# An encoder trunk on one core: the order of each engine's instructions, taken from one scheduling turn and a table of rank changes

## The chip, the cores and the metric

The kernel runs on one core of a Trainium2 chip. A core has five engines with an instruction queue each: TensorE (PE, matrix products), VectorE (DVE), ScalarE (ACT), GpSimd (POOL) and SyncE (SP, which here starts transfers). The metric is the device time of one execution in microseconds (us), lower is better. Of the kernel before there are three timed runs and one profiled execution.

## The reference

Two layers work on an input of 512 rows of 1024 numbers in float32. Each layer normalizes, mixes the rows by attention, normalizes and adds; then it normalizes, runs a gated feed-forward block, normalizes and adds:

```python
for layer in range(2):
    h = rms_norm(x, norm_mix_pre[layer])
    h = neighbourhood_attention(h, ...) if layer == 0 else dilated_attention(h, ...)
    x = x + rms_norm(h, norm_mix_post[layer])
    h = rms_norm(x, norm_ffn_pre[layer])
    x = x + rms_norm(swiglu(h, w_gate, w_up, w_down), norm_ffn_post[layer])
# swiglu(h) = (silu(h @ w_gate) * (h @ w_up)) @ w_down, inner width 2816
```

Layer 0 lays the rows on an 8 x 64 grid; each of 16 heads of 64 attends to a window of 8 grid rows by 16 columns, with a learned bias by relative position. Layer 1 has three attentions side by side, each with its own queries, keys and values: windows of 128, 512 and 2048 over every row, every 4th and every 16th, with a penalty by distance; their outputs are weighted by their softmax denominators and summed.

## The kernel before

**Products.** A float32 product is made of three faster ones: each operand is split into a high part (ScalarE copies it rounded, L437) and a low part (VectorE subtracts, L438), and `mm3` issues high x high, high x low and low x high (L449, L450, L451). Large products are cut into 2 x 2 blocks and made from seven block products ("units") instead of eight. The sums of weight blocks that this needs are made on POOL or VectorE (L517 to L523), their splits on ScalarE and VectorE. ScalarE (L529, L752, L758, L765) and VectorE (L753, L760, L763) read the finished sums from PSUM, the memory where TensorE accumulates.

**Stages of a layer.** q, k and v (products `vp`, `pp_n` in layer 0, `vd`, `pp_d` in layer 1); attention of a pair of heads; the output product `yo`; gate and up products `gu`; the down product `yd`. In between, rows are normalized: ScalarE squares and sums (L708), VectorE multiplies (L709), POOL raises the mean to the power -1/2 (L657), VectorE scales and adds the residual (L715), and the next pre-norm squares on ScalarE (L662), uses POOL's L657 again, and scales on VectorE (L664). `transposed` then turns four 128 x 128 blocks on TensorE into one PSUM bank (L671, `tr_...`), ScalarE copies the high part out (L673) and VectorE the low part (L674). The names `h_a`, `l_a` are the two parts of a weight block, `rxa`, `rxb`, `rxc` the parts of the transposed rows.

**Attention of layer 1.** In a pair `j`, `scores_a` makes the scores of the widest neighbourhoods as split products (`sa`, L1330); `scores_b` makes those of the other two attentions as plain float32 matmuls on 64 rows (`sb`, L1350). A softmax follows (VectorE L1313, ScalarE L1314). ScalarE scales the result by the weights of the three attentions in 128 x 256 pieces (L1400), TensorE transposes them (`t1_j`, L1410), four to a bank; ScalarE copies one bank out and VectorE the next (both L1411). `values` multiplies with v, again in plain float32 (`o1`, L1419). Layer 0 has plain float32 products too (`o`, L845). VectorE also splits the rotated q and k (L774, L780 to L785).

**Buffers.** PSUM has eight banks, in four uses: three for `pp` (units), two for scores, two for transposes ("t"), one for attention outputs. The third tile of a use waits until the readers of the first are done.

**What sets the order.** The code records all instructions and does not run in the order in which it is written. `Order` collects them with their dependences (data, buffers) and a cost of its own for each. `run(rank, back)` is a list scheduler: each of five queues (four engines and SyncE's transfers) takes, whenever it is free, the ready instruction of lowest rank; TensorE prefers to stay with the kind of matmul it is in when a rank is less than 1000 ns behind (`stay`). Run backwards from the end, it gives new ranks. `pin` alternates forward and backward in 20 turns. It then rates the 20 orders with `usual`, the mean length of an order under three draws of random delays; it starts from the best, and for each stretch of 100 us it tries the ranks of 12 other turns and keeps a mixture that rates better. At last it ties each instruction to the one ahead of it on its engine, so the order found at build time is the order on the chip.

Of the kernel before, what the change touches and what calls it, by code (L numbers as in the profile page):

```python
# [70 lines left out]
def _in_psum(b):  # L71
    return list(b.tensor.shape) == [P, 512]
# [6 lines left out]
def _cost(i, e):  # L79
# [8 lines left out]
    if t == "InstDMACopy":  # L88
        adds = "bypass" not in str(getattr(i, "cce_op", "bypass"))
        size = 4 * n * outs[0].ap[0][1] * (1.78 if adds else 1)  # L90
# [9 lines left out]
    if e == 1:  # L100
        f = str(getattr(i, "func", ""))
        if "Exp" in f or "Silu" in f or len(srcs) > 1 and n > 16:
            c = 55 + 1.38 * n
        else:
            c = (48 if _in_psum(srcs[0]) else 80) + 0.86 * n
        c += _scattered(outs[0]) * 0.95 * n
        return (c + 93, c + 290, False, 0, 0) if len(outs) > 1 else (c, c + 100, False, 0, 0)
    if e == 2:
        c, lock = 60 + 1.055 * n, sum(not _in_psum(b) for b in srcs) > 1
        if t == "InstMemset":  # L110
            return 180, 270, False, 0, 0
        if t == "InstTensorCopy":
            lock = not _in_psum(srcs[0])
            c = 60 + (0.53 if lock else 1.055) * n
        elif t == "InstCustomDveAnt":
            c, lock = c + 90, False
        elif t == "InstTensorScalarPtr" and n == D:
            c = 1202
        c += _scattered(outs[0]) * 0.78 * n
        return c, c + 80, lock, 0, 0  # L120
    if e == 3:
        if t == "InstMemset":
            return 30 + n, 60 + n, False, 0, 0
        if t == "InstTensorTensor":
            c = 515 if n == 1 else 90 + 2.28 * n
        else:
            c = 300 + 0.62 * n if t == "InstTensorScalarPtr" else 260
        return c, c + 40, True, 0, 0
    return 100, 100, False, 0, 0


class Order:
# [147 lines left out]
                now = min(q[0] if q is wake else q[0][0] for q in (wake, pending) if q)  # L280
        return starts, order, max(s + max(c[1], c[4] and LANDING + c[4] / RATE) for s, c in zip(starts, self.costs))

    def through(self, order, costs):

        left, ready, at, last = [len(p) for p in self.pred], [0.0] * len(self.all), [0] * 5, 0.0
        free, locked, half, kind, pipe = [0.0] * 5, [0.0] * 5, [0.0] * 2, 0, 0.0
        rest = [e for e in range(5) if order[e]]
        while rest:
            now, e, k = min((max(free[e], ready[order[e][at[e]]]), e, order[e][at[e]]) for e in rest
                            if not left[order[e][at[e]]])  # L290
            taken, later, lock, mode, size = costs[k]
            s = max(now, pipe - AHEAD) if e == 4 else max(now, locked[5 - e]) if lock else now
            if e == 0:
                if mode > 2:
                    s = max(s + SWITCH.get((kind, 3), 0), half[mode - 3])
                    half[mode - 3] = s + later - 200
                else:
                    s = max(s + SWITCH.get((kind, mode), 0), max(half) + 95)
                    taken += 100 * (kind == 3)
                kind = min(mode, 3)  # L300
            if lock:
                locked[e] = s + taken
            if size:
                pipe = max(s + taken, pipe) + size / RATE
                end = pipe + LANDING + later
            else:
                end = s + later
            free[e], last = s + taken, max(last, end)
            for v in self.succ[k]:
                same = self.engine[v] == e and not size  # L310
                ready[v] = max(ready[v], s + taken if same and e == 0 else end if same else end + SYNC)
                left[v] -= 1
            at[e] += 1
            if at[e] == len(order[e]):
                rest.remove(e)
        return last

    def usual(self, order):

        ends = []  # L320
        for seed in range(3):
            r, costs = random.Random(seed), []
            for e, (taken, later, lock, mode, size) in zip(self.engine, self.costs):
                if size:
                    later = r.gauss(300, 700) if size < 4e5 else r.gauss(50, 800)
                    later *= 1.6 if e == 3 else 1
                else:
                    later += r.expovariate(1 / 15)
                costs.append((taken, later, lock, mode, size))
            ends.append(self.through(order, costs))  # L330
        return sum(ends) / len(ends)

    def pin(self, tc, times, span):
        rank, found = list(range(len(self.all))), []

        self.costs = [(t, LATE if 0 < size < 2e4 else later, lock, mode, size) for t, later, lock, mode, size in self.costs]
        for _ in range(times):
            starts, order, end = self.run(rank, False)
            found.append((self.usual(order), end, rank, starts, order))
            starts, _, end = self.run([-s - c[1] for s, c in zip(starts, self.costs)], True)  # L340
            rank = [end - s - c[0] for s, c in zip(starts, self.costs)]
        found.sort(key=lambda f: f[0])

        best, end, rank, base, order = found[0]
        for lo in np.arange(0.0, max(base), span):
            part = [k for k, s in enumerate(base) if lo <= s < lo + span]
            for _, _, other, _, _ in found[1:13]:
                mixed, shift = list(rank), float(np.median([rank[k] - other[k] for k in part]))
                for k in part:
                    mixed[k] = other[k] + shift  # L350
                _, new, e = self.run(mixed, False)
                usual = self.usual(new) if e < end + 3000 else best
                if usual < best:
                    best, end, rank, order = usual, e, mixed, new
        for q in order:
            for m, n in zip(q, q[1:]):
                tc.add_manual_dep(self.all[n], self.all[m].name,
                                  mybir.DependencyInfo(mybir.DependencyClass.NoSync, mybir.DependencyReason.DATA),
                                  reason="order")
# [3 lines left out]
def encoder_kernel(ctx: ExitStack, tc: tile.TileContext, a: dict, out: bass.AP):  # L363
# [1069 lines left out]
    order = [3 * j + g for j in range(PAIRS) for g in orders[j]]  # L1433
    stats, parts, weight, pts, vg, ready, left, later = {}, {}, {}, {}, {}, [], {}, {}

    vus, vslots = {}, cycle([hl(rxc[:, 24:], 0, D), hl(rxs, 2, D), (vmem, rxs[:, 4 * D:])])
    for qd in range(2):
        v = v_quarter(ap[:, (6 + qd) * D:(7 + qd) * D], a["dil_v"][0, qd], f"d{qd}")
# [75 lines left out]
              for n, lo, hi, o, c, side in arenas]  # L1514
    order = Order(tc.nc.cur_bb.bb.instructions)
    order.link(tags, places, extra)
    order.pin(tc, 20, 1e5)


def _blocks(w, cols):  # L1520
# [79 lines left out]
```

## Time and profile before

| | |
|---|---|
| median of 3 runs | 1460.94 us (1460.33 to 1461.76) |
| the profiled execution | 1460.49 us |
| its span, first to last instruction | 1458.7 us |
| TensorE clock granted, mean | 0.997 |
| busy: PE matmul | 1423.1 us, 98% of the span, 10788 instructions |
| busy: PE weight load | 1318.6 us, 90% |
| busy: DVE | 1179.3 us, 81%, 1876 instructions |
| busy: ACT | 902.1 us, 62%, 1819 instructions |
| busy: POOL | 541.0 us, 37%, 398 instructions |
| read from and written to HBM | 229.24 MB and 68.29 MB, 204 GB/s over the span |

The profiled execution's own time is 1.79 us over its span and 0.45 us under the median of the runs. Busy time is the sum of the times in which an engine works on something. The matmul's end is modelled and successive matmuls overlap, so PE can read as fully busy while its starts lie further apart than they need to. The distance between starts is what tells.

### The profile page before, as it was taken

How to read it: one execution, taken by the hardware profiler on the slowest of the kernel's cores; microseconds unless marked ns; L12 is line 12 of the kernel's file. 1: busy time of each engine (PE TensorE's matmuls, PEld its weight loads, DVE VectorE, ACT ScalarE, POOL GpSimd, SP SyncE). 2: the span in 40 equal slices, each digit the busy share in tenths (PEclk: the TensorE clock that was granted, in tenths of full speed). 3: DMA queues.
4: the chain of work that ended last, by engine and by line, in shares of the span. 5: the costliest groups of instructions: out<-in, count | busy, mean ns of one | idle time of the engine just before them, and what ended most of it. 6: DMA issues, size and time to landing. Idle time of an engine off the chain costs nothing.

```text
span 1458.7 us, 27918 instructions
## 1 busy us (share of the span) xinstructions
PE 1423.1 (98%) x10788; PEld 1318.6 (90%) x10788; DVE 1179.3 (81%) x1876; ACT 902.1 (62%) x1819; POOL 541.0 (37%) x398
## 2 busy tenths in 40 slices
PE   7999999999999999999999999999999999999997
PEld 6998877999999888999999999999877999999886
DVE  5499976899999888878678678787667989998877
ACT  4478873655555657544477677887775645555664
POOL 5345524544430001765553433344213644340001
PEclk9999999999999999999999999999999999999999
DMA  5356578788234674445433343343675788944662
GB/s 204 125 196 166 186 249 215 257 240 219 99 117 142 198 231 164 156 154 173 131 105 102 111 139 95 97 146 117 218 222 201 212 213 259 269 151 152 200 218 95
DMA packets 86645, 253.22 MB, mean 174 GB/s; under 512 B 19312, under 2 KB 31600, under 8 KB 84464
## 3 DMA queue, kind: packets, MB, share of 16 engines
q1 hardware_dynamic: 77696, 197.69, 41.0%
q0 software_dynamic: 8672, 53.48, 14.3%
q8 instruction: 85, 1.39, 0.4%
q14 instruction: 48, 0.39, 0.1%
q10 hardware_dynamic: 144, 0.26, 0.0%
HBM read 229.24 MB, written 68.29 MB: 204 GB/s over the span
## 4 chain that ended last, share of the span: by engine, by line
PE 82%; DVE 7%; ACT 5%; issue 2%; DMA 1%; POOL 1%; SPq 0%; POOLq 0%; DVEq 0%; ACTq 0%
PE gu L449 9%; PE gu L450 9%; PE gu L451 9%; PE pp_d L449 4%; PE pp_d L450 4%; PE pp_d L451 4%; PE yd_s L451 3%; PE yd_s L449 3%; PE yd_s L450 3%; PE vd L449 2%; PE vd L450 2%; PE vd L451 2%; PE yd_pp L451 2%; PE yd_pp L449 2%; PE yd_pp L450 2%
## 5 line engine op out<-in xcount | busy, mean ns | idle before, releaser
L657 POOL TENSOR_TENSOR rs_yd<-v_yd,mhalf 128x1 f32<-128x1 f32 x8 | 13.2, 1654 | 259.0 <-DVE v_yd L655 259.0
L450 PE MATMUL gu<-rxc,h_a 128*128 128x256 f32 x352 | 98.9, 281 | 1.3 <-DVE rxc L674 1.3
L449 PE MATMUL gu<-rxc,h_a 128*128 128x256 f32 x352 | 98.4, 280 | 1.0 <-ACT h_a L437 0.7
L449 PE MATMUL gu<-rxa,h_c 128*128 128x256 f32 x352 | 98.6, 280 | 0.6 <-DVE mem L915 0.4
L451 PE MATMUL gu<-rxc,l_a 128*128 128x256 f32 x352 | 98.6, 280 | 0.1
L449 PE MATMUL gu<-rxa,h_b 128*128 128x256 f32 x352 | 97.9, 278 | 0.1
L451 PE MATMUL gu<-rxa,l_b 128*128 128x256 f32 x352 | 97.7, 278 | 0.2 <-DVE l_b L438 0.2
L450 PE MATMUL gu<-rxa,h_b 128*128 128x256 f32 x352 | 97.8, 278 | 0.0
L450 PE MATMUL gu<-rxa,h_c 128*128 128x256 f32 x352 | 97.6, 278 | 0.0
L451 PE MATMUL gu<-rxa,l_c 128*128 128x256 f32 x352 | 97.4, 278 | 0.0
L517 POOL TENSOR_TENSOR r_d<-r_d 128x512 f32<-128x512 f32 x24 | 35.2, 1465 | 163.3 <-DVE l_ad L438 131.3
L437 ACT ACTIVATE rxc<-mem 128x512 fp32r<-128x512 f32 (+2 forms) x90 | 55.7, 623 | 60.7 <-PE yd_pp L450 32.0
L517 POOL TENSOR_TENSOR r_gu<-r_gu 128x512 f32<-128x512 f32 x20 | 33.3, 1666 | 153.0 <-DVE l_a L438 79.4
L438 DVE TENSOR_TENSOR rxc<-mem,rxc 128x512 fp32r<-128x512 f32 (+2 forms) x90 | 64.9, 727 | 16.8 <-ACT rxc L437 16.6
L517 POOL TENSOR_TENSOR raw<-raw 128x512 f32<-128x512 f32 x24 | 40.7, 1696 | 76.2 <-DVE l_a L438 73.5
L450 PEld LDWEIGHTS gu<-rxc,h_a 128*128 128x128 f32 x352 | 66.9, 190 | 1.7 <-DVE rxc L674 1.7
L449 PEld LDWEIGHTS gu<-rxc,h_a 128*128 128x128 f32 x352 | 66.8, 190 | 1.5 <-ACT h_a L437 1.0
L449 PEld LDWEIGHTS gu<-rxa,h_c 128*128 128x128 f32 x352 | 66.2, 188 | 1.6 <-DVE mem L915 0.6
L451 PEld LDWEIGHTS gu<-rxc,l_a 128*128 128x128 f32 x352 | 66.8, 190 | 0.3 <-DVE l_a L438 0.3
L449 PEld LDWEIGHTS gu<-rxa,h_b 128*128 128x128 f32 x352 | 66.3, 188 | 0.4 <-ACT h_b L437 0.3
L451 PEld LDWEIGHTS gu<-rxa,l_b 128*128 128x128 f32 x352 | 66.2, 188 | 0.4 <-DVE l_b L438 0.4
L450 PEld LDWEIGHTS gu<-rxa,h_b 128*128 128x128 f32 x352 | 66.2, 188 | 0.3 <-DVE rxa L674 0.2
(609 smaller groups left out, 6114.2 us busy)
## 6 DMA issues: line engine op xcount, KB each, us to landing
wsum<-wd POOLq DMA_DIRECT2D x24, 1408.0 KB, 11.9
r_d<-dil_qk SPq DMA_DIRECT2D x48, 512.0 KB, 4.0
raw<-wg SPq DMA_DIRECT2D x24, 512.0 KB, 5.0
raw<-wu SPq DMA_DIRECT2D x24, 512.0 KB, 7.0
wsum<-wsum POOLq DMA_DIRECT2D x8, 1408.0 KB, 10.5
raw<-wsum SPq DMA_DIRECT2D x22, 512.0 KB, 4.3
r_gu<-wg SPq DMA_DIRECT2D x20, 512.0 KB, 4.8
r_gu<-wu SPq DMA_DIRECT2D x20, 512.0 KB, 5.6
```

The lines of the kernel that those rows point to most:

```text
L437: act.activation(h, src, AF.Copy)
L438: dve.tensor_sub(l, src, h.bitcast(F32))
L449: i = pe.matmul(o, s[0], m[0], start=start, stop=False, skip_group_check=True)
L450: pe.matmul(o, s[0], m[1], start=False, stop=False, skip_group_check=True)
L451: pe.matmul(o, s[1], m[0], start=False, stop=stop, skip_group_check=True)
L517: self.added = e[0].tensor_add(q[0], q[0], q[2])
L657: pool.tensor_tensor(r, v, mhalf, op=ALU.pow)
```

## The change

The rating of orders is gone from the build: `through`, `usual` and the mixing by stretches. `pin` still makes 20 turns. It then takes the ranks of turn 5 and edits them by a table of 80 rows `(what, engine, lo, hi, turn, by)`. A row picks instructions of one engine (0 is PE, 1 ACT, 2 DVE; 5 is all) by their start in turn 5 (`what` 0 and 1, ns) or by their number (`what` 2). It adds `by` to their rank, or, for `what` 0, puts turn `turn`'s rank plus `by` in its place. One run of the scheduler with the edited ranks gives the order, which is tied as before. No instruction, transfer, buffer or dependence of the program's own is added or taken away.

```diff
-    def through(self, order, costs):
...
-    def usual(self, order):
...
+FIRST, TABLE = 5, (
+    (1, 0, 543664, 559242, 0, 1876), (2, 0, 5180, 5342, 0, 4228), (1, 0, 1022772, 1028275, 0, 1433),
...
-    def pin(self, tc, times, span):
+    def pin(self, tc, times, first, table):
...
-            starts, order, end = self.run(rank, False)
-            found.append((self.usual(order), end, rank, starts, order))
-            starts, _, end = self.run([-s - c[1] for s, c in zip(starts, self.costs)], True)
+            starts, _, end = self.run(rank, False)
+            found.append((rank, starts))
+            starts, _, _ = self.run([-s - c[1] for s, c in zip(starts, self.costs)], True)
             rank = [end - s - c[0] for s, c in zip(starts, self.costs)]
-        found.sort(key=lambda f: f[0])
-
-        best, end, rank, base, order = found[0]
-        for lo in np.arange(0.0, max(base), span):
-            part = [k for k, s in enumerate(base) if lo <= s < lo + span]
-            for _, _, other, _, _ in found[1:13]:
-                mixed, shift = list(rank), float(np.median([rank[k] - other[k] for k in part]))
-                for k in part:
-                    mixed[k] = other[k] + shift
-                _, new, e = self.run(mixed, False)
-                usual = self.usual(new) if e < end + 3000 else best
-                if usual < best:
-                    best, end, rank, order = usual, e, mixed, new
+
+        rank, base = list(found[first][0]), found[first][1]
+        for what, e, lo, hi, turn, by in table:
+            for k, s in enumerate(base):
+                if e in (5, self.engine[k]) and lo <= (k if what == 2 else s) < hi:
+                    rank[k] = by + (found[turn][0][k] if what == 0 else rank[k])
+        order = self.run(rank, False)[1]
...
-    order.pin(tc, 20, 1e5)
+    order.pin(tc, 20, FIRST, TABLE)
```

What it moves is seen in the order itself. A row below is a line of the source, the operation, out<-in and the shape; "x4" is four in a row. Lines of the changed source are 23 lower (L671 is L648 there, L449 to L451 are L426 to L428, L1410 is L1387). PE's first 131 and last 447 instructions stand as before; between them nearly every stretch differs, mostly by a few microseconds of work.

**First place: from the output product to the gate product of layer 0.** On PE, before; `yo0_3_1` is the last output block, `tr_o0_...` are transposes of normalized rows, `gu0_...` gate and up units:

```order
L449 MATMUL yo0_3_1_2708<-rxb0_92,rxa_77 128x512
L450 MATMUL yo0_3_1_2708<-rxb0_92,rxa_77 128x512
L451 MATMUL yo0_3_1_2708<-rxb0_92,rxa_77 128x512
L671 MATMUL tr_o0_0_0_2616<-ident_69,mem_79 128x128 x4
L671 MATMUL tr_o0_0_1_2623<-ident_69,mem_79 128x128 x4
L671 MATMUL tr_o0_1_0_2630<-ident_69,mem_79 128x128 x4
L671 MATMUL tr_o0_1_1_2637<-ident_69,mem_79 128x128 x4
L449 MATMUL gu0_0_2861<-rxc_78,h_a0_0_2862 128x256
L449 MATMUL gu0_1_2896<-rxc_78,h_a0_1_2897 128x256
L449 MATMUL gu0_2_2930<-rxc_78,h_a0_2_2931 128x256
L450 MATMUL gu0_0_2861<-rxc_78,h_a0_0_2862 128x256
L451 MATMUL gu0_0_2861<-rxc_78,l_a0_0_2863 128x256
```

The same on PE in the changed kernel:

```order
L426 MATMUL yo0_3_1_2708<-rxb0_92,rxa_77 128x512
L648 MATMUL tr_o0_0_0_2616<-ident_69,mem_79 128x128 x4
L648 MATMUL tr_o0_0_1_2623<-ident_69,mem_79 128x128 x2
L427 MATMUL yo0_3_1_2708<-rxb0_92,rxa_77 128x512
L428 MATMUL yo0_3_1_2708<-rxb0_92,rxa_77 128x512
L648 MATMUL tr_o0_0_1_2623<-ident_69,mem_79 128x128 x2
L648 MATMUL tr_o0_1_0_2630<-ident_69,mem_79 128x128 x4
L426 MATMUL gu0_0_2861<-rxc_78,h_a0_0_2862 128x256
L648 MATMUL tr_o0_1_1_2637<-ident_69,mem_79 128x128 x4
L426 MATMUL gu0_1_2896<-rxc_78,h_a0_1_2897 128x256
L427 MATMUL gu0_0_2861<-rxc_78,h_a0_0_2862 128x256
L428 MATMUL gu0_0_2861<-rxc_78,l_a0_0_2863 128x256
```

Two of the last output matmuls now stand behind the first transposes, and the first matmul of `gu0_2` no longer stands ahead of the rest of `gu0_0`: it follows 54 matmuls later.

On DVE at the same place, before:

```order
L674 TENSOR_TENSOR rxc_78<-tr_o0_0_0_2616,rxc_78 128x4x128
L709 TENSOR_TENSOR mem_79<-yo0_3_1_2708,mem_79 128x512
L674 TENSOR_TENSOR rxc_78<-tr_o0_0_1_2623,rxc_78 128x4x128
L715 SCALAR_TENSOR_TENSOR mem_79<-mem_79,few_small_80 128x1024
L674 TENSOR_TENSOR rxc_78<-tr_o0_1_0_2630,rxc_78 128x4x128
L674 TENSOR_TENSOR rxc_78<-tr_o0_1_1_2637,rxc_78 128x4x128
L438 TENSOR_TENSOR l_a0_2_2932<-raw0_2857,h_a0_2_2931 128x1024
```

And in the changed kernel:

```order
L651 TENSOR_TENSOR rxc_78<-tr_o0_0_0_2616,rxc_78 128x4x128
L632 TENSOR_SCALAR few_small_80<-few_small_80 128x1
L686 TENSOR_TENSOR mem_79<-yo0_3_1_2708,mem_79 128x512
L651 TENSOR_TENSOR rxc_78<-tr_o0_0_1_2623,rxc_78 128x4x128
L651 TENSOR_TENSOR rxc_78<-tr_o0_1_0_2630,rxc_78 128x4x128
L692 SCALAR_TENSOR_TENSOR mem_79<-mem_79,few_small_80 128x1024
L651 TENSOR_TENSOR rxc_78<-tr_o0_1_1_2637,rxc_78 128x4x128
L630 TENSOR_SCALAR few_small_80<-few_small_80 128x1
L641 SCALAR_TENSOR_TENSOR mem_79<-mem_79,few_small_80 128x1024
L415 TENSOR_TENSOR l_a0_2_2932<-raw0_2857,h_a0_2_2931 128x1024
```

The third low-part copy (of `tr_o0_1_0`) now stands ahead of the residual step (L715 before, L692 now), and the low part of the weight block `l_a0_2` behind the pre-norm's L664 (now L641). On POOL the L657 that the residual step needs has moved ahead of two 128 x 512 sums (L699, L701).

**Second place: pair 3 of layer 1's attention, about 882 us.** On PE, before; `sb_3_...` are plain float32 scores, `t1_2_...` transposes of pair 2, `pp_d14` a unit:

```order
L1350 MATMUL sb_3_0_1_9673<-mem_79 128x128 x2
L1410 MATMUL t1_2_9541<-ident_69,mem_79 128x128
L1410 MATMUL t1_2_9547<-ident_69,mem_79 128x128
L1410 MATMUL t1_2_9541<-ident_69,mem_79 128x128 x3
L1410 MATMUL t1_2_9547<-ident_69,mem_79 128x128 x3
L1350 MATMUL sb_3_0_1_9673<-mem_79 128x128 x2
L449 MATMUL pp_d14_9822<-rxa_77,h_ad14_9846 128x256
L1410 MATMUL t1_2_9609<-ident_69,mem_79 128x128
L1350 MATMUL sb_3_1_1_9674<-mem_79 128x128 x4
```

In the changed kernel:

```order
L1387 MATMUL t1_2_9541<-ident_69,mem_79 128x128 x4
L1327 MATMUL sb_3_0_1_9673<-mem_79 128x128 x4
L427 MATMUL pp_d14_9822<-rxa_77,h_ad14_9846 128x256
L428 MATMUL pp_d14_9822<-rxa_77,l_ad14_9847 128x256
L1387 MATMUL t1_2_9547<-ident_69,mem_79 128x128 x4
L1387 MATMUL t1_2_9609<-ident_69,mem_79 128x128
```

The scores of `sb_3_0_1` stand in one run instead of two; those of `sb_3_1_1` still make one of their own further on. Counted over the whole program, PE's plain float32 matmuls (`sb`, `o`, `o1`) stand in 76 separate runs before and 61 now: 26 and 22 for `sb`, 30 and 21 for `o1`, 20 and 18 for `o`. Runs of transposes number 108 and 112.

**Third place: pair 4, about 970 us.** On ACT, before; L1400 are the scalings, L1411 the copy out of a transpose bank, L778 and L779 q and k:

```order
L1400 ACTIVATE mem_79<-mem_79 128x256 x7
L1411 COPY mem_79<-t1_4_10626 128x512
L1400 ACTIVATE mem_79<-mem_79 128x256 x2
L778 ACTIVATE rxc_78<-memc0_2853 64x512
L1400 ACTIVATE mem_79<-mem_79 128x256 x3
L1411 COPY mem_79<-t1_4_10642 128x512
L779 ACTIVATE rxc_78<-memc0_2853 64x512
```

In the changed kernel:

```order
L1377 ACTIVATE mem_79<-mem_79 128x256 x8
L1388 COPY mem_79<-t1_4_10626 128x512
L1377 ACTIVATE mem_79<-mem_79 128x256 x2
L755 ACTIVATE rxc_78<-memc0_2853 64x512
L756 ACTIVATE rxc_78<-memc0_2853 64x512
L1377 ACTIVATE mem_79<-mem_79 128x256 x3
L1388 COPY mem_79<-t1_4_10642 128x512
```

Ahead of the copy of `t1_4_10642` stand, counted from the start of the program, three more scalings (the piece shows one of them), and L779. On PE the first transpose of `t1_4_10710`, which is the next to use the bank that this copy frees, follows the last transpose of `t1_4_10642` after 9 unit matmuls and six `sb` ones; before, after 37 and eight. Over all 32 such copies, counted from the start, 11 now have one to four more scalings ahead of them (24 in sum), 19 as many as before and 2 one fewer.

More of the change, by code (lines that the diff above doesn't have):

```diff
@@ L1 @@
 import heapq
-import random
 from contextlib import ExitStack, contextmanager
@@ L129, in _cost @@
     return 100, 100, False, 0, 0
+FIRST, TABLE = 5, (
[27 rows of a table added]
+)
 class Order:
@@ L281, in run @@
         return starts, order, max(s + max(c[1], c[4] and LANDING + c[4] / RATE) for s, c in zip(starts, self.costs))
-    def through(self, order, costs):
[L285 to L316, printed above, removed]
@@ L318, in usual @@
-    def usual(self, order):
[L320 to L331, printed above, removed]
```

26 rows, old and new, of the table c are left out of this document.

## The prediction

> **What bounds the kernel now.** I read the page's busy line and its chain first, then TensorE's waits, then PE's timeline, for the distances between starts.
>
> ```profile
> span 1458.7 us, 27918 instructions
> PE 1423.1 (98%) x10788; PEld 1318.6 (90%) x10788; DVE 1179.3 (81%) x1876; ACT 902.1 (62%) x1819; POOL 541.0 (37%) x398
> PE 82%; DVE 7%; ACT 5%; issue 2%; DMA 1%; POOL 1%; SPq 0%; POOLq 0%; DVEq 0%; ACTq 0%
> ...
> PE tr_a L671 <- DVE mem L664: 8.6, 2, 8.2
> PE sa L1330 <- DVE mem L1313: 1.3, 1, 1.3
> PE yo L449 <- DVE mn L817: 1.2, 1, 1.2
> ...
> PE s L805 <- POOL rxc L1199: 0.7, 1, 0.7
> ```
>
> PE is busy in 98% of the span and carries 82% of the chain. The waits (total us, times, longest) are small: the largest, 8.6, lies mostly ahead of the first transpose, where PE's order stays. No work goes away, so what an order can win is a few us: these waits, and distances between starts that the kind of neighbour sets. It can lose any amount, by new waits. 1% would be 14.6 us.
>
> **Term 1: fewer switches into plain float32.** PE's plain float32 matmuls (`sb`, `o`, `o1`) stand in 61 runs, not 76. What a run costs, PE's timeline shows (two trace rows per such matmul, so x4 is two matmuls and x8 four):
>
> ```profile
> 881.46 0.28 PE L450 MATMUL pp_d<-rxa,h_ad 128*128 128x256 f32 x1
> 881.57 0.28 PE L451 MATMUL pp_d<-rxa,l_ad 128*128 128x256 f32 x1
> 881.78 0.71 PE L1350 MATMUL sb<-mem 64*128 64x128 f32 x4
> ...
> 884.79 1.16 PE L1350 MATMUL sb<-mem 64*128 64x128 f32 x8
> 885.88 0.66 PE L1410 MATMUL t<-ident,mem 128*128 128x128 f32 x4
> ...
> 970.16 0.71 PE L1350 MATMUL sb<-mem 64*128 64x128 f32 x4
> 970.79 0.39 PE L451 MATMUL pp_d<-rxa,l_cd 128*128 128x256 f32 x1
> ```
>
> Unit matmuls start 0.11 apart (881.46, 881.57); into the float32 run it takes 0.21, so entering costs 0.10. Two matmuls hold PE from 970.16 to 970.79, 0.63; four from 884.79 to 885.88, 1.09. So one costs 0.23, and 1.09 - 4 x 0.23 = 0.17 is for leaving. A run costs 0.27. Output products leave more dearly:
>
> ```profile
> 197.65 0.54 PE L845 MATMUL o<-mem 128*64 128x192 f32 x2 [0.29 <-ACT mem L835]
> 198.12 0.50 PE L449 MATMUL yo<-h_wo,rxa 128*128 128x512 f32 x1
> ```
>
> One matmul takes 0.47 to the next start; less the 0.23 of the other shape (the nearest row), 0.24, so with entry 0.34 a run. Of the 15 runs fewer, 4 are `sb`, 11 outputs: 4 x 0.27 + 11 x 0.34 = 4.8. I take 15 x 0.30 = **-4.5**; ends 15 x 0.27 = 4.1 and 15 x 0.34 = 5.1. The four more runs of transposes I take at nothing: at 0.10 for an entry they would cost 0.4 at most. PE is the bound around these places, so the whole counts, unless PE would wait there anyway: then nothing.
>
> **Term 2: waits with more room.** The best shown is the way from the output product to the gate product of layer 0, from PE, DVE and POOL:
>
> ```profile
> 254.67 0.65 PE L671 MATMUL tr_o<-ident,mem 128*128 128x128 f32 x4 [1.18 <-DVE rxc L674]
> 255.87 0.66 PE L671 MATMUL tr_o<-ident,mem 128*128 128x128 f32 x4 [0.54 <-DVE rxc L674]
> 257.51 0.38 PE L449 MATMUL gu<-rxc,h_a 128*128 128x256 f32 x1 [0.75 <-ACT h_a L437]
> 258.67 0.58 PE L450 MATMUL gu<-rxc,h_a 128*128 128x256 f32 x1 [0.77 <-DVE rxc L674]
> ...
> 253.93 0.69 DVE L674 TENSOR_TENSOR rxc<-tr_o,rxc 128x512 fp32r<-128x512 f32 x1 [0.27 <-ACT rxc L673]
> 256.72 1.28 DVE L715 SCALAR_TENSOR_TENSOR mem<-mem,few_small 128x1024 f32<-128x1024 f32 x1 [0.91 <-POOL few_small L657]
> 257.93 1.28 DVE L674 TENSOR_TENSOR rxc<-tr_o,rxc 128x512 fp32r<-128x512 f32 x2
> 261.97 2.31 DVE L664 SCALAR_TENSOR_TENSOR mem<-mem,few_small 128x1024 f32<-128x1024 f32 x1 [0.44 <-POOL few_small L657]
> ...
> 256.14 0.55 POOL L657 TENSOR_TENSOR few_small<-few_small,mhalf 128x1 f32<-128x1 f32 x1
> ```
>
> The last number in brackets is PE's idle time and who ended it: 1.18, 0.54, 0.75 and 0.77. PE resumes at 258.67 when the copy of `tr_o0_1_0` is done, which stood behind L715, which waited for POOL. In the new order `tr_o0_0_0` starts two 512-wide matmuls earlier (0.23 each, 0.45); its L673, L674 follow at 253.5, L674 ends at 254.15, `tr_o0_1_0` goes at 254.2. On DVE come L709, L674 and then at once L674 of `tr_o0_1_0`, 0.6 apart: it ends near 256.2. So `gu0_0` goes on at 256.3, not 258.67, and 23 matmuls of `gu0_0` and `gu0_1` are at hand before `gu0_2` is asked for: about **-2.2**, after 0.1 to 0.2 for `gu0_2`'s moved matmul. What is late next: `l_a0_2` now stands behind L664 (2.31), but its user comes about 6 us after 256.3, and POOL's L657 comes two sums earlier, which brings L715 and L664 forward. The two sums themselves come 0.55 later (L657's time), and their transposes stand further back. Ends: -3.2 (all four waits) and 0.
>
> The others, by PE's idle times:
>
> ```profile
> 200.19 0.33 PE L830 MATMUL ta<-ident,mem 128*128 128x128 f32 x1 [0.65 <-POOL mem L1215]
> 737.71 0.35 PE L1330 MATMUL sa<-rxc 128*128 128x256 f32 x1 [1.27 <-DVE mem L1313]
> 751.98 0.39 PE L449 MATMUL pp_d<-rxa,h_cd 128*128 128x256 f32 x1 [0.46 <-DVE mem L763]
> 774.27 0.38 PE L451 MATMUL pp_d<-rxa,l_ad 128*128 128x256 f32 x1 [0.73 <-DVE l_ad L438]
> 779.05 0.39 PE L449 MATMUL pp_d<-rxa,h_cd 128*128 128x256 f32 x1 [0.30 <-DVE mem L763]
> 820.87 0.39 PE L449 MATMUL pp_d<-rxb,h_cd 128*128 128x256 f32 x1 [0.32 <-DVE mem L760]
> 1124.35 0.38 PE L450 MATMUL gu<-rxc,h_a 128*128 128x256 f32 x1 [0.51 <-DVE rxc L674]
> ```
>
> - End of layer 0's attention (197.65, 200.19): output matmuls now stand as filler ahead of both waits: -0.9 (0.29 + 0.65).
> - 738: more units stand ahead of `sa`, so its wait for the score bank goes, but L774, which it needs too, now stands behind a split on DVE: I take -0.5 of 1.27.
> - 752, 774, 779, 820: the producer named (L763, or `l_ad`) moves up on DVE, or a dozen unit matmuls come ahead: -1.5 of 1.81.
> - 1124, the same passage as the first, in layer 1: here L709 and L715 move ahead of the copies on DVE, the other way: +0.4, between a later wait gone (about 0.7) and 1.28 more.
>
> Sum: -2.2 - 0.9 - 0.5 - 1.5 + 0.4 = **-4.7**; ends -7.3 (all of these waits but the last) and 0.
>
> **Term 3: new waits in layer 1's attention.** Eleven of the 32 copies of a transpose bank by ACT now have more scalings ahead, 24 in sum. ACT's timeline:
>
> ```profile
> 969.33 1.29 ACT L1400 ACTIVATE mem<-mem 128x256 f32<-128x256 f32 x3
> 970.53 0.56 ACT L1411 COPY mem<-t 128x512 f32<-128x512 f32 x1
> 971.12 0.63 ACT L779 ACTIVATE rxc<-memc 64x512 fp32r<-64x512 f32 x1
> 976.27 1.06 ACT L437 ACTIVATE h_ad<-r_d 128x1024 fp32r<-128x1024 f32 x1
> ```
>
> Three scalings take 1.20 to the next start, 0.40 each. If PE waited for each one, 24 x 0.40 = 9.6. Behind a late copy on PE stand the next transposes, which need its bank, and all units behind them. Place by place it is less. About 882, four more scalings (1.6) stand ahead of the copy, but PE has unit matmuls and `sb` between the transposes, so ACT is done in time: 0. About 970, from the first scaling, ACT needs 8 x 0.40, 0.56 for each of two copies, and 0.6 each for L778 and L779, ending near 5.5 (3.2 + 0.56 + 0.6 + 0.6 + 0.56); PE is at `t1_4_10710` after 3.8, because 28 of 37 unit matmuls that stood between are now elsewhere: 1.7 late. Two more places of two and three scalings (925 to 935, 1061) I could not resolve; 5 x 0.40 = 2.0. Together I take **+3.7**; ends 0 and 9.6. It is nearest to the 970 row, the one traced by hand.
>
> **Sum.** -4.5 - 4.7 + 3.7 = -5.5. Against the profiled execution, 1460.49 (span 1458.7 and 1.79 around it), that is 1455.0; the median lies 0.45 higher: **1455.4**. What a measurement of this kernel can tell from no change is about 0.2%, 2.9 us: faster is below 1458.0, slower above 1463.9.
>
> **Rivals.**
> - *ACT falls behind in attention (slower).* The late copies cost the whole 9.6, and since ACT is in order, what stands behind (such as L437, 1.06 at 976.27) is late too, once in each of the four pairs: 9.6 + 4.2 = 13.8. With terms 1 and 2, -9.2: 1460.94 + 4.6 = 1465.5. It decides when the new waits exceed 9.2 + 2.9 = 12.1, 3.0 for each pair. For it: these pairs' copies moved one way, 11 later, 2 earlier. Against: ACT is busy 62% of the span and can work ahead where PE has units to do. 0.15.
> - *The savings come back as waits (no change).* Term 1 stands, but where a wait is shortened PE meets the next producer: DVE is 81% busy, and moving one step up puts another back. Term 2 comes to 0: 1460.94 - 4.5 + 3.7 = 1460.1. 0.22.
> - *DVE and POOL meet elsewhere.* In layer 0's first units DVE steps stretch beside POOL's sums:
>
> ```profile
> 82.45 2.06 DVE L784 TENSOR_TENSOR akl<-mem,rxc 64x512 fp32r<-64x512 f32 x1
> 89.34 0.69 DVE L785 TENSOR_TENSOR akl<-mem,rxc 64x512 fp32r<-64x512 f32 x1
> 82.66 1.30 POOL L519 TENSOR_TENSOR r_n<-r_n 128x512 f32<-128x512 f32 x1
> 88.85 0.39 PE L805 MATMUL s<-rxc 128*128 128x256 f32 x1 [0.68 <-POOL rxc L1199]
> ```
>
>  The same shape took 2.06 beside a sum and 0.69 alone, 1.37 more, and it stands in the chain to the first scores. That chain moves ahead of other splits on DVE, so it may miss POOL's sums; what PE can win is its wait there, 0.68: 1455.4 - 0.7 = 1454.7. Met once more, 1455.4 + 1.4 = 1456.8. 0.10 for the first. The Trainium skill ("SBUF — State Buffer", Who interferes with whom) says that a DVE step with two SBUF inputs and a GpSimd step that reads SBUF exclude each other for a whole instruction; by that rule such a meeting would cost up to the sum's own time, and the trace agrees roughly, 1.37 beside 1.30.
>
> That nothing moves is excluded: PE's order differs from its 132nd instruction on.
>
> **How the numbers follow.** Forecast 0.53, rivals 0.15, 0.22, 0.10. Faster is nearly all of the forecast and the third, some of the second: 0.48 + 0.10 + 0.05, **0.63**. Slower: most of the first and the tail of the second, **0.17**. Same: **0.20**. Low end: no new waits, the best ends of terms 1 and 2, and the wait of `yo` for L817 gone as well, 1460.94 - 5.1 - 7.3 - 1.2 = 1447.3. High end reaches the first rival: 1465. The forecast's own range is 1450 to 1459.
>
> **What would show it.** Right: PE's starts near 256.3 where 258.67 stood, with the L715 row behind L674; fewer entries into `sb` and `o1`; the 0.3 to 0.7 waits of `pp_d` shorter. Wrong: a row of `t` or `o1` on PE waiting over 1 us for ACT's L1388 (L1411 before) or its scalings; PE's busy time unchanged.

## The result, and the profile after

The changed kernel takes 1452.09 us (median of 4 runs, 1450.34 to 1452.58), the kernel before in the same comparison 1461.35 (1460.33 to 1462.1): a ratio of 0.9934, with a 95% interval of 0.9918 to 0.9950. It is faster by 9.3 us; the forecast was 5.5. The profiled execution took 1450.34, the shortest of the four, so its trace shows a little more than the medians do: 10.1 us less span.

The page, and from the list of PE's waits (total us, times, longest) the ones that are new or larger:

```profile
span 1448.6 us, 27907 instructions
PE 1415.8 (98%) x10788; PEld 1315.1 (91%) x10788; DVE 1178.2 (81%) x1876; ACT 902.6 (62%) x1819; POOL 543.0 (37%) x398
PE 82%; ACT 6%; DVE 5%; DMA 4%; issue 1%; POOL 0%; SPq 0%; POOLq 0%; DVEq 0%; ACTq 0%
...
PE tr_o L648 <- DVE rxc L651: 2.3, 3, 1.2
PE gu L427 <- DVE rxc L651: 2.2, 1, 2.2
...
PE vd L427 <- DVE rxc L415: 1.3, 1, 1.3
```

The busy shares say nothing: PE reads 98% in both. So I cut both traces at the same eight matmuls (ones with the same number of PE instructions ahead of them, to within three) and compared the stretches. Two of them, from the busy times by stretch, before and after (stretch, length, busy time of PE, PEld, DVE, ACT, POOL, granted clock, DMA share, GB/s):

```profile
725.52:1110.16 384.64, 379.50 (x3125) 345.57 (x3124) 282.96 (x625) 279.63 (x714) 143.20 (x104) 1.00 0.44 138
1110.16:1150.62 40.46, 38.87 (x282) 35.48 (x281) 36.21 (x50) 25.55 (x49) 28.96 (x23) 1.00 0.49 169
```

```profile
723.15:1097.23 374.08, 371.66 (x3123) 342.70 (x3121) 284.04 (x624) 279.04 (x711) 139.68 (x102) 1.00 0.46 141
1097.23:1142.63 45.40, 40.92 (x282) 37.53 (x281) 35.87 (x52) 26.13 (x49) 28.98 (x23) 0.92 0.47 179
```

The same matmuls of layer 1's attention take 374.08 instead of 384.64 us, and those of the passage behind it 45.40 instead of 40.46. All stretches, with what the forecast's terms put there (a run of float32 at 0.30):

| stretch (times before) | before | after | difference | forecast |
|---|---|---|---|---|
| start to 217.56, attention of layer 0 | 217.56 | 216.80 | -0.8 | -1.5 |
| to 278.73, passage to the gate product, layer 0 | 61.17 | 56.28 | -4.9 | -2.2 |
| to 584.43, gate, up and down, layer 0 | 305.70 | 307.25 | +1.5 | 0 |
| to 645.20, v of layer 1, first half | 60.77 | 62.25 | +1.5 | 0 |
| to 725.52, v, second half | 80.32 | 80.57 | +0.2 | 0 |
| to 1110.16, attention of layer 1 | 384.64 | 374.08 | -10.6 | -2.2 |
| to 1150.62, passage, layer 1 | 40.46 | 45.40 | +4.9 | +0.4 |
| to the end | 308.08 | 305.97 | -2.1 | 0 |

A row can be out by the three matmuls, some 0.7 us: cut at exactly equal numbers, the first two rows read -1.5 and -4.1. One trace is also one execution. Nine of the kernels below keep the order of gate, up and down of layer 0, and seven of them take 0.3 to 1.3 us less there than this trace, so most of that +1.5 is scatter.

A second cut of the same traces sorts PE's starts by what stands ahead of them. I take for each pair of neighbouring matmuls the usual distance from start to start (the 30th percentile of that kind of pair in both traces) and sum it over the program. It falls by 4.3 to 5.3, by how finely kinds are told apart (by shape, line or tile): fewer switches. What starts over 0.15 later than usual falls by 3.6 to 4.7: waits, and stretches of slow clock (last section). The first transpose is 0.4 earlier; the rest is under 1.5.

The first place, in PE's, DVE's and POOL's timeline after:

```profile
252.56 0.66 PE L648 MATMUL tr_o<-ident,mem 128*128 128x128 f32 x4 [0.59 <-DVE rxc L651]
253.90 0.39 PE L426 MATMUL gu<-rxc,h_a 128*128 128x256 f32 x1 [0.69 <-ACT rxc L650]
254.68 0.33 PE L427 MATMUL gu<-rxc,h_a 128*128 128x256 f32 x1
254.85 0.28 PE L428 MATMUL gu<-rxc,l_a 128*128 128x256 f32 x1
...
253.29 1.28 DVE L651 TENSOR_TENSOR rxc<-tr_o,rxc 128x512 fp32r<-128x512 f32 x2
254.49 1.27 DVE L692 SCALAR_TENSOR_TENSOR mem<-mem,few_small 128x1024 f32<-128x1024 f32 x1
...
252.87 0.55 POOL L634 TENSOR_TENSOR few_small<-few_small,mhalf 128x1 f32<-128x1 f32 x1
```

POOL's power step is done at 253.4, DVE makes the low part of `tr_o0_1_0` before the residual step, and PE goes on with `gu0_0` at 254.68, where 258.67 stood. Two idle times are left of four.

In layer 1 the same passage still has POOL's old order, and DVE's residual step now stands ahead of two copies:

```profile
1112.85 0.48 PE L426 MATMUL gu<-rxc,h_a 128*128 128x256 f32 x1 [0.52 <-ACT h_a L414]
1115.53 0.58 PE L427 MATMUL gu<-rxc,h_a 128*128 128x256 f32 x1 [2.21 <-DVE rxc L651]
...
1113.59 1.28 DVE L692 SCALAR_TENSOR_TENSOR mem<-mem,few_small 128x1024 f32<-128x1024 f32 x1 [2.21 <-POOL few_small L634]
...
1111.77 1.28 POOL L676 TENSOR_TENSOR mem<-mem 128x512 f32<-128x512 f32 x1
1113.00 0.56 POOL L634 TENSOR_TENSOR few_small<-few_small,mhalf 128x1 f32<-128x1 f32 x1
```

POOL's power step stands behind four sums, DVE's residual step waits 2.21 for it, the copy that PE needs stands behind that, and PE waits the same 2.21. That is the longest of its kind: in the six other kernels below that keep this order, the same wait reads 0.75 to 1.66.

### The profile page after: what moved, and what is told of

Read it like the earlier page. It is cut to its first block, busy times and chain, and to the rows that moved or that the text cites. A ratio compares the mean times of both kernels' runs of the same rounds, so it can differ in the third digit from the quotient of the medians.

```text
span 1448.6 us, 27907 instructions
## 1 busy us (share of the span) xinstructions
PE 1415.8 (98%) x10788; PEld 1315.1 (91%) x10788; DVE 1178.2 (81%) x1876; ACT 902.6 (62%) x1819; POOL 543.0 (37%) x398
## 3 DMA queue, kind: packets, MB, share of 16 engines
q0 software_dynamic: 8672, 53.48, 14.3%
## 4 chain that ended last, share of the span: by engine, by line
PE 82%; ACT 6%; DVE 5%; DMA 4%; issue 1%; POOL 0%; SPq 0%; POOLq 0%; DVEq 0%; ACTq 0%
PE gu L426 10%; PE gu L427 10%; PE gu L428 10%; PE pp_d L426 4%; PE pp_d L427 4%; PE pp_d L428 4%; PE yd_s L427 3%; PE yd_s L426 3%; PE yd_s L428 3%; PE vd L427 2%; PE vd L426 2%; PE vd L428 2%; PE yd_pp L428 2%; PE yd_pp L426 2%; PE yd_pp L427 2%; ACT mem L1377 2%
## 5 line engine op out<-in xcount | busy, mean ns | idle before, releaser
L426 PE MATMUL gu<-rxc,h_a 128*128 128x256 f32 x352 | 98.6, 282 | 1.2 <-ACT rxc L650 0.7
L428 PE MATMUL gu<-rxc,l_a 128*128 128x256 f32 x352 | 98.5, 281 | 0.0
L426 PE MATMUL gu<-rxa,h_c 128*128 128x256 f32 x352 | 98.2, 280 | 0.0
L426 PE MATMUL gu<-rxa,h_b 128*128 128x256 f32 x352 | 97.9, 278 | 0.0
L428 PE MATMUL gu<-rxa,l_b 128*128 128x256 f32 x352 | 97.8, 278 | 0.0
L428 PE MATMUL gu<-rxa,l_c 128*128 128x256 f32 x352 | 97.3, 278 | 0.0
L426 PEld LDWEIGHTS gu<-rxc,h_a 128*128 128x128 f32 x352 | 66.8, 190 | 1.7 <-ACT rxc L650 0.9
L506 ACT ACTIVATE mem<-gu 128x256 f32<-128x256 f32 x44 | 16.9, 383 | 81.8 <-PE gu L428 77.5
L428 PEld LDWEIGHTS gu<-rxc,l_a 128*128 128x128 f32 x352 | 67.2, 191 | 0.0
L426 PEld LDWEIGHTS gu<-rxa,h_c 128*128 128x128 f32 x352 | 66.1, 188 | 1.0 <-DVE mem L894 0.4
L427 PEld LDWEIGHTS gu<-rxa,h_b 128*128 128x128 f32 x352 | 66.2, 188 | 0.2 <-DVE rxa L651 0.2
L428 PEld LDWEIGHTS gu<-rxa,l_b 128*128 128x128 f32 x352 | 66.3, 188 | 0.1
```

Of the source, the lines that this page charges most:

```text
L426: i = pe.matmul(o, s[0], m[0], start=start, stop=False, skip_group_check=True)
L427: pe.matmul(o, s[0], m[1], start=False, stop=False, skip_group_check=True)
L428: pe.matmul(o, s[1], m[0], start=False, stop=stop, skip_group_check=True)
L506: act.activation(self.p5, self.right, AF.Copy)
```

## The experiments

Each kernel ran beside the kernel before on one chip; its ratio to that is what compares across the table, since the median of before moved between 1460.75 and 1461.92. Where two intervals overlap, the difference is unclear. "Against" is the median less 1452.09, or for the one built from before, less its own 1461.92.

| kernel | median (range) | ratio to before, 95% | against |
|---|---|---|---|
| the changed kernel | 1452.09 | 0.9934 (0.9918 to 0.9950) | |
| split_runs | 1465.52 (1465.07 to 1467.15) | 1.0031 (1.0019 to 1.0043) | +13.4 |
| merge_before | 1465.14 (1461.39 to 1467.96) | 1.0022 (1.0012 to 1.0032) | +3.2 |
| copies_later | 1458.58 (1455.3 to 1467.13) | 0.9993 (0.9979 to 1.0008) | +6.5 |
| copies_back | 1460.92 (1457.31 to 1463.34) | 0.9992 (0.9983 to 1.0001) | +8.8 |
| passage0_back | 1457.02 (1453.97 to 1459.83) | 0.9970 (0.9958 to 0.9983) | +4.9 |
| passage1 | 1449.76 (1449.08 to 1451.23) | 0.9923 (0.9910 to 0.9936) | -2.3 |
| passage1_all | 1449.66 (1446.06 to 1452.52) | 0.9916 (0.9902 to 0.9930) | -2.4 |
| vd_first | 1451.42 (1449.81 to 1452.75) | 0.9934 (0.9921 to 0.9946) | -0.7 |
| x_later | 1451.06 (1449.18 to 1452.61) | 0.9926 (0.9914 to 0.9938) | -1.0 |
| no_table | 1474.63 (1471.52 to 1475.98) | 1.0089 (1.0075 to 1.0103) | +22.5 |
| best | 1445.08 (1444.75 to 1445.78) | 0.9888 (0.9873 to 0.9902) | -7.0 |

All but one edit the finished order; a pair of numbers in a diff means "the first instruction goes right ahead of the second on its engine".

```diff
-        order = self.run(rank, False)[1]
+        order = self.edited(self.run(rank, False)[1])
```

### Does a run of float32 cost 0.3?

**split_runs**: 40 runs cut in two by the next unit matmul.

```diff
+    self.split_runs(order, 40)   # new = q[:mid] + [next unit matmul] + q[mid:]
```

> The changed kernel with 40 of its runs of plain float32 matmuls on PE cut in two: the first unit matmul behind a run moves into its middle, so that there are 101 runs instead of 61; nothing else moves. Theory A (a run costs PE 0.27 to 0.34 us for entering and leaving, and PE is the bound around it): slower by 40 x 0.30 = 12 us than the changed kernel, about 1464, near or above the kernel before. Rival (PE would wait at these places anyway, so the 15 runs fewer explain little): slower by less than 4 us, below 1456.

It came to +13.4, 0.34 a run, waits behind the cuts included: theory A. PE's timeline, one run in the changed kernel and the same one cut:

```profile
876.63 1.16 PE L1327 MATMUL sb<-mem 64*128 64x128 f32 x8
877.72 0.39 PE L427 MATMUL pp_d<-rxa,h_ad 128*128 128x256 f32 x1
```

```profile
886.34 0.71 PE L1327 MATMUL sb<-mem 64*128 64x128 f32 x4
886.97 0.38 PE L427 MATMUL pp_d<-rxa,h_ad 128*128 128x256 f32 x1
887.29 0.71 PE L1327 MATMUL sb<-mem 64*128 64x128 f32 x4
887.92 0.38 PE L428 MATMUL pp_d<-rxa,l_ad 128*128 128x256 f32 x1
```

Four float32 matmuls take 1.09 in one piece; in two, 0.63 each, and the unit matmul between them takes 0.32 to the next start, instead of 0.11.

**merge_before**: in the kernel before, the second of two near runs moved up to the first, 76 runs to 62.

```diff
-        for q in order:
+        for q in self.edited(order):   # self.merge_runs(order, 12)
```

> The kernel before with one thing done to it: where two runs of plain float32 matmuls on PE stand no more than 12 instructions apart, the second is moved up to the first as far as the dependences allow, so that there are 62 runs instead of 76; the matmuls between them follow. Theory A (a run costs 0.30 to 0.34): faster than the kernel before by 14 x 0.3 = 4.2 to 4.8 us, about 1456.4, less what the moved matmuls wait for their operands. Rival (the runs fewer only go along with the better order): within 1.5 us of the kernel before.

Slower by 3.2, against both. The usual distances fell by 4.0 to 4.4, as theory A had it. But what starts over 0.15 late rose by 7.6 to 7.9; PE's idle times over 0.15, taken from 12 us on, rose from 16.6 to 20.8. Two of them in PE's timeline:

```profile
805.34 0.90 PE L1350 MATMUL sb<-mem 64*128 64x128 f32 x7 [0.74 <-DVE mem L1313]
...
1061.23 1.62 PE L1419 MATMUL o<-mem 128*64 128x256 f32 x15 [0.97 <-ACT mem L1411]
```

Pulled ahead, the scores wait for the bank that DVE still reads (L1313), the output product for ACT's copy. Behind the second the clock also read 0.50 from 1067.6 to 1071.0. So the price of a run is real, but a run saved by moving work ahead of its producers is paid back. The table's order moves the producers as well: by the same count its idle times fell from 16.6 to 14.3.

### Did the late copies on ACT cost anything?

**copies_later** moves ACT's copies out of the transpose banks back past 53 further scalings. **copies_back** gives 13 copies as many scalings ahead as before: 11 move forward, by 24 places, and two back by one.

```diff
+    self.copies(order, 4)          # copies_later: each copy behind up to 4 more scalings
+    self.copies(order, places)     # copies_back: as many scalings ahead as in the kernel before
```

> The changed kernel with ACT's copies out of the transpose banks in layer 1's attention moved further back: each of the 32 stands behind up to four more scalings, as far as the data dependences allow, 53 places in all. Theory A (ACT works ahead of PE there, so the copies have room): within 2 us of the changed kernel. Theory B (the prediction's third term, 3.7 us for 24 places, 0.15 each): slower by 8 us, about 1460. Theory C (PE waits for each scaling, 0.40 each): slower by 21 us.

> The changed kernel with ACT's copies out of the transpose banks in layer 1's attention put back to as many scalings ahead of them as before (26 places in 13 copies); the rest stays new. Theory A (the new order only uses up room that was there; the profile of the changed kernel shows waits of 0.2 us at two of these transposes and 0.71 behind them at 967): within 1.5 us of the changed kernel, 1450.5 to 1453.5. Theory B (each place costs 0.15, as in the prediction and as in the run with the copies moved still further back): faster by 3.7 us, about 1448.4.

copies_later cost 6.5, near theory B's 8. ACT's and PE's timeline there:

```profile
958.07 4.09 ACT L1377 ACTIVATE mem<-mem 128x256 f32<-128x256 f32 x10
...
964.17 0.56 ACT L1388 COPY mem<-t 128x512 f32<-128x512 f32 x1
...
964.79 0.98 PE L1387 MATMUL t<-ident,mem 128*128 128x128 f32 x7 [2.23 <-ACT mem L1388]
```

That is the wait which the forecast feared: PE's idle times ahead of these transposes sum to 6.8 here, and to 0.2 in the changed kernel. The one idle time over 0.3 near them there is 0.55, at 967.71, and ends with another step of ACT (L506). The room for the 24 places was there, and the next 53 overdraw it.

copies_back brought neither theory B's gain of 3.7 nor theory A's standstill: it cost 8.8. ACT and PE:

```profile
1054.66 0.59 ACT L1388 COPY mem<-t 128x512 f32<-128x512 f32 x1 [3.22 <-PE t L1387]
...
1058.79 0.44 PE L1307 MATMUL sa<-rxc 128*128 128x256 f32 x1 [3.93 <-DVE rxc L751]
...
922.59 1.16 PE L1327 MATMUL sb<-mem 64*128 64x128 f32 x8 [1.29 <-DVE mem L1290]
```

Seen from ACT, PE's transposes come later in the new order. In the kernel before, with as many scalings ahead, ACT waited 0.24 at one of these copies and less than 0.15 at the others; in copies_back it waits at five of the eleven for the transposes, 6.7 in sum. A copy put back to its old place stands at the head of ACT's queue, and behind the longest of these waits, 3.22, stand the exponentials and the splits of q and k, DVE's low part behind those, and PE, idle for 3.93. The last line is a wait near two others of the five. Around this wait the clock read 0.50 too, from 1058.9 to 1062.3. So the late copies are no cost that the table took: with PE's new order they are needed.

### The two passages

**passage0_back** undoes DVE's and POOL's part in layer 0; **passage1** does it in layer 1; **passage1_all** adds the orders of PE and ACT there.

```diff
+    # passage0_back: residual step ahead of the copy, power step behind two sums
+    self.moved(order, (("I-2803", "I-2636"), ("I-2802", "I-2807")))
+    # passage1: the copy ahead of the residual step, the power step ahead of three sums
+    self.moved(order, (("I-12312", "I-12485"), ("I-12484", "I-12444")))
+    # passage1_all: also six transposes ahead of two yo matmuls, gu1_2's first matmul later, ACT to match
+    self.moved(order, (..., ("I-12293", "I-12434"), ("I-12617", "I-12618"), ("I-12297", "I-12481"), ...))
```

> The changed kernel with two instructions put back at the passage from the output product to the gate product of layer 0: on DVE the residual step stands ahead of the third low-part copy, and on POOL the power step behind the two sums, both as before; PE's and ACT's orders stay new. Theory A (these two orders carry the gain there; PE would go on after about 257.9 instead of 254.6): slower by 2.5 to 3.3 us, about 1455. Rival (the gain there came from PE's order, the transposes ahead of the last output matmuls): slower by less than 1 us.

> The changed kernel with two instructions moved at the passage from the output product to the gate product of layer 1: on DVE the third low-part copy stands ahead of the residual step, and on POOL the power step that the residual step needs stands ahead of three sums, as it already is in layer 0 there. Theory A (PE's wait of 2.21 us at 1115.53 is this order): faster by about 2.3 us than the changed kernel, about 1449.8. Rival (the next producer, the weight block's split or its transfer, takes the wait over): within 0.7 us.

> The changed kernel with the whole passage from the output to the gate product of layer 1 ordered as the table orders it in layer 0: besides the two moves on DVE and POOL also PE's first transposes ahead of the last two output matmuls, the first matmul of the third gate unit behind the others, and ACT's and DVE's copies to match. Theory A (the waits of 1.18, 0.54, 0.52 and 2.21 us on PE there are this order, each as in layer 0 before): faster than the changed kernel by 3.5 to 4.2 us, about 1448.2, and by 1.2 to 1.9 than with the two moves alone. Rival (the order of DVE and POOL is all): as with the two moves alone, about 1449.8.

PE in the first two:

```profile
259.75 0.58 PE L427 MATMUL gu<-rxc,h_a 128*128 128x256 f32 x1 [3.13 <-DVE rxc L651]
260.12 0.42 PE L428 MATMUL gu<-rxc,l_a 128*128 128x256 f32 x1
260.34 0.41 PE L426 MATMUL gu<-rxc,h_a 128*128 128x256 f32 x1
```

```profile
1115.40 0.39 PE L426 MATMUL gu<-rxc,h_a 128*128 128x256 f32 x1 [0.69 <-ACT h_a L414]
1115.62 0.28 PE L427 MATMUL gu<-rxc,h_a 128*128 128x256 f32 x1
1115.74 0.28 PE L428 MATMUL gu<-rxc,l_a 128*128 128x256 f32 x1
```

Undone, there is one wait of 3.13, and the run costs 4.9, more than the wait and more than theory A's 2.5 to 3.3: behind it the matmuls start 0.21 to 0.22 apart, not 0.11. Done in layer 1, the wait of 2.21 is gone and the passage is 2.9 shorter. The median gives -2.3, which is theory A's figure, but by the ratios it is 1.6 and the intervals overlap; the span of this profile is the changed kernel's own, 1448.6, because other stretches, whose order stayed, took as much longer (two of them 1.6 and 1.4). So the gain is shown at its place and unclear in the whole. Of passage1_all's further 1.2 to 1.9 the median shows nothing (-0.1), with a wide spread. Its profile is of its longest run: `yo` waits 2.16 there for ACT's split `wm` at 216, the first transposes of the passage wait 2.54, and the clock reads 0.50 for 6.8 us behind them. The last kernel, with the same order in the passage, shows 0.59 and no slow clock there. What decides between the two stays open.

### The v products, the residual rows, the table

**vd_first** moves the split that PE waits for ahead of the one that POOL waits for; **x_later** moves four loads on SP's queue; **no_table** leaves out the table's rows.

```diff
+    self.moved(order, (("I-6905", "I-6990"), ("I-6906", "I-6991")))                      # vd_first
+    self.moved(order, tuple((x, "I-2859") for x in ("I-2796", "I-2590", "I-2599", "I-2694")))  # x_later
-        for what, e, lo, hi, turn, by in table:
+        for what, e, lo, hi, turn, by in ():                                              # no_table
```

> The changed kernel with two steps moved in layer 1's v products (about 632 to 640 us): the split of the block that PE waits for next (ACT's high part, DVE's low part) stands ahead of that of the block which POOL sums next. In the changed kernel's profile DVE's L415 took 3.27 us there, of which 2.2 lie beside a POOL sum, and PE then waits 1.30 us for the split behind it. Theory A (that order makes PE's wait): faster by 1.3 to 1.5 us. Rival (POOL's next sum comes 2 us later and PE then waits for it instead): within 0.5 us or slower.

> The changed kernel with four loads of the residual rows on SP's queue (at 205 to 211 us, first used at 229.75) moved behind the two weight loads that follow them; nothing else. PE waits 0.23 us for ACT's split wm at 213.6 in one profiled execution and 1.45 in another, and ACT there waits for the store of the attention output, which shares the queues with these loads. Theory A (the store comes later the more loads run beside it): faster by 0.2 to 1.2 us, and a narrower spread between runs. Rival (the store's time does not hang on them): within 0.3 us.

> The changed kernel with the ranks of turn 5 alone, no row of the table. Theory A (the gain lies in the table's local moves; a turn by itself is no better than the mixture before): 1458 to 1466, near the kernel before. Rival (the choice of the turn carries most of the gain): below 1455.

The place in the changed kernel, POOL, DVE and PE, and PE in vd_first:

```profile
632.42 2.42 POOL L562 TENSOR_TENSOR r_dv<-r_dv,r_dv 128x1024 f32<-128x1024 f32 x1
...
632.65 3.27 DVE L415 TENSOR_TENSOR l_ad<-mem,h_ad 128x1024 fp32r<-128x1024 f32 x1 [0.26 <-ACT h_ad L414]
...
639.53 0.39 PE L427 MATMUL vd<-rxc,rxb 128*128 128x256 f32 x1 [1.30 <-DVE rxc L415]
```

```profile
640.23 0.39 PE L426 MATMUL vd<-h_dd,rxa 128*128 128x256 f32 x1 [0.84 <-DVE mem L594]
```

The wait of 1.30 went and another of 0.84 came, for the DVE sum that now stood behind. The gain of 0.7 is inside both intervals, and the ratio is the changed kernel's: unclear, and nearer to the rival. x_later's -1.0 is inside them too. Without the table, turn 5 alone is slower than the kernel before by 0.89%, and slower still than theory A's 1458 to 1466: the gain of the change is the table's.

### The version from all of it

**best**: passage1_all, vd_first with the sum ahead of the other split, and x_later.

> The changed kernel with the whole passage of layer 1 ordered as in layer 0, the split in the v products first (with DVE's sum L594 ahead of the other split, since PE waited 0.84 us for it where only the split was moved), and the residual rows' loads later. Theory A (the waits are at different places and add): faster than the changed kernel by 3.8 + 0.7 to 1.5 + 0.2 to 1.2, so 1445.6 to 1447.4. Rival (what one place gives is lost at the next, as where float32 runs were merged): not below 1448.

1445.08, ratio 0.9888 (0.9873 to 0.9902): faster than the changed kernel, whose interval begins at 0.9918, by 7.0 where 4.7 to 6.5 were expected, and than before by 16.5. The page's span, and what is left of the two kinds of waits:

```profile
span 1443.5 us, 27909 instructions
...
PE tr_o L648 <- DVE rxa L651: 1.5, 2, 0.8
PE gu L426 <- ACT rxc L650: 1.4, 2, 0.7
PE tr_o L648 <- DVE rxc L651: 1.2, 2, 0.6
```

Its profile has no slow clock in layer 1's passage, 3.2 us less there than the changed kernel's, and 1.6 less in the v products. PE does not wait for `wm` near 214 (0.2 to 2.2 us in seven of the nine other profiles with the new order), and the four runs lie within 1.0 us. That the loads' place does it was not settled by x_later alone, whose profile still has a wait of 0.79 there.

## Why the prediction held, point by point

- **Term 1, -4.5: right**, in size (-4.3 to -5.3 by distances, 0.34 a run by split_runs). Its condition, "unless PE would wait there anyway", weighs more than the text gave it: merge_before lost there all that it saved.
- **Term 2, the first place, -2.2: the step was right, the sum too small.** `gu0_0` was put at 256.3; the trace runs 1.5 earlier by then (a matmul of `yo0_2_0` at 237.57 stands at 236.03), so 254.8 is meant, and 254.68 came. But the stretch gained 4.9 (4.1 when cut at equal numbers). PE's idle times fell by 2.0, from 3.24 to 1.28. What was left out is how long PE is slow behind a cluster of waits (below): 13 matmuls near 260 started 0.21 apart before, 0.10 more than usual each. passage0_back, which undoes DVE's and POOL's part alone, loses 4.9.
- **Term 2, the same passage in layer 1, +0.4: the mis-sized term.** It took the order on DVE and not what the residual step waits for, POOL's power step behind four sums. The stretch lost 4.9: 2.21 on that wait in this trace (0.75 to 1.66 in six others), and again a slow clock, 18 matmuls of 0.10. passage1's passage is 2.9 shorter.
- **Term 3, +3.7: wrong, in sign.** The count of scalings ahead of ACT's copies was right, and copies_later shows the mechanism at work once there is no room. The failed step is to count scalings as if PE's transposes stayed where they were for ACT: they come later too, and copies_back shows that copies left in place would cost 8.8. The attention stretch, forecast at -2.2, gave -10.6. Runs are -4.4 of it, at 0.34 for 13 of the 15; PE's idle times, 4.6 before and 2.2 after, are -2.4, nearly all between 728 and 820. The remaining 3.8 lie in starts that come late without such an idle time, and were not followed further.
- **Not in the sum:** +1.5 in the v products, where DVE meets a POOL sum, which the third rival named for another place (best, which changes the order there, has the 1.5 back); -2.1 from layer 1's gate product to the end, not followed; +1.5 in layer 0's gate, up and down products, mostly scatter as said.
- **The rivals:** the first (ACT falls behind) did not come: no row of `t` or `o1` on PE waits over 1 us, the prediction's own sign of being wrong; copies_later is what it would have looked like. The second (paid back as waits) describes merge_before and vd_first, and in the changed kernel layer 1's passage. That the sum was out by less than its terms is luck in part: the +3.7 that did not come and the 4.5 that layer 1's passage cost beyond its +0.4 lay on opposite sides.

## What to carry to other kernels

When orders of several engines move together, price a step by where its producer and its consumer stand now, not by how far it moved: a copy further back on ACT cost nothing and was needed, because the transposes that feed it came later as well. Follow each wait for a critical copy back through the queues to its start: a step of 0.55 us on POOL behind four sums held two engines for 2.2 us, and two instructions moved made the passage 2.9 us shorter. Here a run of plain float32 matmuls between others costs 0.3 us, but runs are worth joining only where all that the joined work needs is ready.

## What the runs showed of the hardware

**A cluster of waits halves PE's clock for a while.** Windows of 2 us in the changed kernel (the number ahead of the last two is the granted clock):

```profile
1113.00:1115.00 2.00, 0.33 (x1) 0.03 (x1) 1.41 (x2) 0.32 (x2) 0.56 (x2) 0.50 1.04 422
1115.00:1117.00 2.00, 1.47 (x7) 1.47 (x8) 2.00 (x3) 2.00 (x3) 0.00 (x0) 0.50 1.00 365
1117.00:1119.00 2.00, 2.00 (x11) 2.00 (x11) 1.56 (x4) 0.06 (x1) 1.65 (x2) 0.50 0.97 391
1119.00:1121.00 2.00, 2.00 (x16) 2.00 (x16) 2.00 (x1) 0.65 (x1) 2.00 (x2) 0.79 0.08 27
```

PE idled 1.18, 0.54, 0.52 and 2.21 us between 1109 and 1115.5. The clock read 0.50 from 1113.0, so the first three were enough, until 1119.8, with 11 matmuls in 2 us instead of 20. In the kernel before, 1.18, 0.54, 0.75 and 0.77 at the first place did the same from 258.4 to 261.8. All six other kernels with the same order in layer 1's passage show it too; in passage1, 1.18, 0.54 and 0.69 did not lower it, so the sum of the waits alone does not decide. In all these traces a low stretch behind waits lasts 3.41 or 6.83 us. In these two the slow matmuls add some 0.4 us to each microsecond of idle time (1.8 to 4.45, 1.3 to 3.24). The Trainium skill ("TensorE: Matmul & The Clock Gate", Part 1: The HAM clock gate) names a half clock after an idle window of about 3.4 us, and 3.4 us of work to lift it. The half clock agrees, and roughly the time to lift it: 3.2 and 4.3 us from the end of the last wait. But no idle time ahead of these two falls was longer than 1.18, so broken idle time can be enough.

**A DVE split that meets a POOL sum can stand still until the sum is over.** The split at 632.65 took 3.27: POOL's sum ran to 634.84, 2.19 later, and such a split alone takes 1.21, which would make 3.40. This is the lock that the Trainium skill ("SBUF — State Buffer", Who interferes with whom) describes, and the trace agrees. The sum began 0.23 ahead of the split; vd_first, which changes the order around it, showed no clear gain.
